# One reciprocal root per up-projection tile on VectorE's side, and TensorE transposes for the second pieces of the latent heads

## The chip, the core and the metric

One core of a Trainium2 chip runs the whole kernel: TensorE (PE; its weight loads are listed as PEld), VectorE (DVE), ScalarE (ACT), GpSimd (POOL) and the SyncE queue (SP), which here issues every transfer. Each engine takes its instructions in the order in which the built program has them. The metric is the time of one execution in device microseconds (us); lower is better. L with a number is a line of the kernel before.

## The reference

One encoder layer over 1024 positions of width 1024. The part that matters is the latent attention (eight heads, keys and queries of 96 values, of which the last 32 are rotated by position):

```
q = jnp.dot(rmsnorm(q_lat, g_q_latent[l]), w_q_up[l]).reshape(B, S, MLA_HEADS, MLA_QK)
kv = jnp.dot(rmsnorm(kv_lat, g_kv_latent[l]), w_kv_up[l]).reshape(B, S, MLA_HEADS, MLA_NOPE + MLA_V)
k_nope, v = kv[..., :MLA_NOPE], kv[..., MLA_NOPE:]
k = jnp.concatenate(
    [k_nope, jnp.broadcast_to(k_rope[:, :, None, :], (B, S, MLA_HEADS, MLA_ROPE))], axis=-1)
q = rmsnorm(q, g_mla_q[l])
k = rmsnorm(k, g_mla_k[l])
q = jnp.concatenate([q[..., :MLA_NOPE], rope(q[..., MLA_NOPE:], positions)], axis=-1)
...
o_mla = mla_attention(q, k, v)
```

`mla_attention` is a causal softmax by chunks of 64 positions: block i of 128 queries sees the keys of blocks 0 to i. A second attention (eight heads, a band of nine chunks, called the chunk heads here) runs beside it; both outputs meet in the output projection, and a gated MLP with a convolution follows.

## The kernel before

The layer runs in stages: input projections and modulation, the chunk heads, the latent heads, output projection, MLP. Positions are cut in eight tiles of 128 (t or i = 0 to 7).

*Precision.* A float32 factor is split in a high and a low part and multiplied in three passes (`gemm3`). Probabilities are split in two f16 parts, each multiplied with the values.

*Up projections* (`f_up`, L519 on). For each of two groups of four heads (gr = 0, 1) and each t: matmuls `qu` into PSUM, copied to SBUF (`uqr`, L553), squared (`usq`, L555), summed by DVE per head (`uss`, L558), and `rsqrt_mean` (L113 to L116) makes the reciprocal root of the mean on POOL in two steps: scale and add (L115), power of -0.5 (L116). DVE multiplies (`qn`, L561) and `rope_apply` rotates the last 32 values in four POOL steps (L467 to L470), with `uqr` for the products. Then matmuls `ku`, and the same for the key: copy `kraw` (L569), the value's two f16 parts (L571, L572), square (L574), sum (`kss`, L577), the rotary part's own sum added by POOL (L578), a second `rsqrt_mean`, DVE for the first 64 values (L581) and POOL for the rotary 32 (L582). `uqr` and `kraw` come from the tag "R", a ring of four buffers.

*Heads* (`Unit`, `mla_unit`). A head has two units, g = 0 for tiles 0 to 3 and g = 1 for tiles 4 to 7. `prep` makes the unit's query and key pages: `qk_page` (L615 on) transposes four blocks on PE into the PSUM tag "T", which has one buffer (TB = 1), and ACT and DVE write the high and low parts. `scores(i)` computes scores into the PSUM tag "S" (two buffers, L658), DVE masks 64x64 of them (L676) and takes the row minimum (L677; signs are turned), ACT takes the exponential (`Pm`, L683) with its sum, DVE the reciprocal (L685, L686). For n keys, `pieces` is one piece up to 640 and two above (0 to 512, 512 to n): tiles 5, 6 and 7 have second pieces of 256, 384 and 512 columns. Each piece goes the same way: POOL scales it to f16 (`hlm`, L71), DVE makes the low part (L703), and a DMA transpose on SP (L705) turns both into `PTm`. The tags "HL" and "PT" have three buffers each. `values(i)` (L716) multiplies all blocks of `PTm` with the values into one PSUM bank per unit; after four tiles ACT and DVE write the unit's output (L723, L724), which goes to memory.

*What sets the order.* The program is emitted in a loop over tiles: `scores` of tile n, then `values` of tile n - 3 (DEPTH = 3), with steps of other work (`fillers`) taken between by `pace`. The fillers are, in order, the projections of the chunk heads, the latent projections, `f_up(0)`, `f_up(1)` and `f_oca`, which projects the chunk heads' output in sixteen tiles (`oc`; loads `cl` and `wor`). A unit of group 0 with g = 1 and all of group 1 need `f_up(1)` done. A scheduler then reorders what is emitted on each engine by dependencies and priorities (`high_priority`). The buffers of a tag go round in the order in which the program asks for them, whatever the scheduler does. The chunk heads' values take the tag "v16", six buffers, which nothing uses once those heads are done. The tiles `P` wider than 640 come from the tag "pg", six buffers, which also hold the latent pages `latT`.

Of the kernel before, what the change touches and what calls it, by code (L numbers as in the profile page):

```python
# [62 lines left out]
def layer_kernel(ctx, tc, I, out):  # L63
# [49 lines left out]
    def rsqrt_mean(r, ss, n, cols=None):  # L113
        sc = ss if cols is None else ss[:, cols]
        pool.tensor_scalar(sc, sc, 1.0 / n, EPS, op0=MUL, op1=ADD)  # L115
        pool.tensor_tensor(r, ss, nhalf[:].to_broadcast(list(r.shape)), op=ALU.pow)  # L116
# [17 lines left out]
    def rtile(name, shape=(P, 512), dt=F32):  # L134
        return apg.tile(list(shape), dt, name=name, tag="R", bufs=4)
# [322 lines left out]

    latT = {}

    def rope_apply(o, x, tab, t, nh, tmp):

        a = tmp[:, 0:nh * 32].rearrange("p (a b) -> p a b", a=nh)
        b = tmp[:, nh * 32:2 * nh * 32].rearrange("p (a b) -> p a b", a=nh)
        ct = tab[:, t:t + 1, 0:32].to_broadcast([P, nh, 32])
        sn = tab[:, t:t + 1, 32:64].to_broadcast([P, nh, 32])
        pool.tensor_tensor(a, x, ct, op=MUL)  # L467
        pool.tensor_tensor(b, x, sn, op=MUL)
        pool.tensor_tensor(o[:, :, 0:16], a[:, :, 0:16], b[:, :, 16:32], op=SUB)
        pool.tensor_tensor(o[:, :, 16:32], a[:, :, 16:32], b[:, :, 0:16], op=ADD)  # L470

    def f_m():
        w = load_w("wm_", I["w_m"], NM)
# [43 lines left out]
    def f_up(gr):  # L517
        if gr == 0:
            right.__exit__(None, None, None)  # L519
            for i in "4v3":  # L520
                G["cm" + i] = tc.tile_pool(name="gp" + i, bufs=1, side="right", reuse_waits="tile")
                G[i] = G["cm" + i].__enter__()
        wq = []
        for k in range(2):
            raw = qtile(f"wqr{gr}_{k}")
            sp.dma_start(raw[:, :384], I["w_qu"][gr][:, k, :])
            w = g4([P, 2, 512], F32R, f"wq{gr}_{k}")
            hi_of("a", w[:, 0, :384], raw[:, :384])
# [12 lines left out]
        lo_of("p", wk[:, 1], raw[:], wk[:, 0])  # L541
        for t in range(NT):
            h, j = divmod(t, 4)
            sl = slice(j * P, (j + 1) * P)
            if t % 2 == 0:
                mq[gr, t // 2] = g3([P, 2, 4, QK], F32, f"qn{gr}_{t}")
                mk[gr, t // 2] = g3([P, 2, 4, QK], F32, f"kn{gr}_{t}")
                mv[gr, t // 2] = G["v"].tile([P, 2, 4, 2, 64], F16, name=f"vt{gr}_{t}", tag="Gv", bufs=8)
            pt = ps.tile([P, 512], F32, name=f"qu{gr}_{t}", tag="mm", bufs=2)
            yield from gemm3_f(pt[:, :384], [(latT[k, h][:, 0, sl], latT[k, h][:, 1, sl], wq[k][:, 0, :384], wq[k][:, 1, :384])  # L550
                                for k in range(2)])
            raw = rtile(f"uqr{gr}_{t}")
            act.activation(raw[:, :384], pt[:, :384], AF.Copy)  # L553
            sq = qtile(f"usq{gr}_{t}")
            act.activation(sq[:, :384], raw[:, :384], AF.Square)  # L555
            ss = cst.tile([P, 4], F32, name=f"uss{gr}_{t}", tag="ss", bufs=4)
            r = cst.tile([P, 4], F32, name=f"ur{gr}_{t}", tag="rr", bufs=4)
# [15 lines left out]
            s3 = raw[:, 256:512].rearrange("p (a b) -> p a b", a=4)  # L573
            act.activation(s3, r3, AF.Square)  # L574
            ss = cst.tile([P, 4], F32, name=f"kss{gr}_{t}", tag="ss", bufs=4)
            r = cst.tile([P, 4], F32, name=f"kr{gr}_{t}", tag="rr", bufs=4)
            dve.tensor_reduce(ss[:], s3, axis=AX.X, op=ADD)  # L577
            pool.tensor_tensor(ss[:], ss[:], ssr[:, t:t + 1].to_broadcast([P, 4]), op=ADD)  # L578
            rsqrt_mean(r[:], ss[:], QK)
            k_t = mk[gr, t // 2][:, t % 2]  # L580
            dve.tensor_tensor(k_t[:, :, 0:NOPE], r3, r[:].unsqueeze(2).to_broadcast([P, 4, NOPE]), op=MUL)  # L581
            pool.tensor_tensor(k_t[:, :, NOPE:], kr[:, t:t + 1, :].to_broadcast([P, 4, ROPE]),  # L582
                               r[:].unsqueeze(2).to_broadcast([P, 4, ROPE]), op=MUL)


    def load_wo(k0, n, he, le):
# [41 lines left out]
    class Unit:  # L628
# [7 lines left out]
        def scores(u, i):  # L636
# [47 lines left out]
            with tc.high_priority(offset=OFF_P):  # L684
# [2 lines left out]
                u.pt[i] = []  # L687
                for x, (p0, p1) in enumerate(pieces):
                    w = p1 - p0
                    hl = at.tile([P, 1280], F16, name=f"hl{nm}_{x}", tag="HL", bufs=HL_BUFS)  # L690
                    pp = pr[:, p0:p1]
                    cnt[0] += 1
                    mode = (MODE_C if u.band else MODE_M)[cnt[0] % 4]
# [4 lines left out]
                    else:  # L698
# [2 lines left out]
                        else:  # L701
                            act.activation(hl[:, :w], pp, AF.Copy, scale=ri[:])
                        dve.scalar_tensor_tensor(hl[:, w:2 * w], pp, ri[:], hl[:, :w], op0=MUL, op1=SUB)  # L703
# [448 lines left out]
```

## Time and profile before

| what | value |
|---|---|
| median of 3 runs | 1462.71 us (1461.91 to 1462.82) |
| the profiled execution | 1464.36 us |
| its span, first to last instruction | 1462.2 us |
| mean granted TensorE clock | 0.934 |
| busy in the span | PE 87%, DVE 69%, POOL 56%, ACT 42% |
| first and last copy of an up projection (L553) | 400.9 and 489.5 us |
| first and last score matmul of the latent heads (L658) | 429.9 and 656.9 us |
| DMA transposes of the latent heads (L705) | 88, median 3.3 us from issue to landing |

A row of a group gives line, engine, operation, output and inputs, shapes, count, then busy time, mean of one in ns, and the idle time before it with what ended it. A row of waits gives who waited for whom, the sum in us, how often, and the longest. A row of the timeline gives start and length in us. A busy PE is not a PE at its peak, since matmuls overlap.

### The profile page before, as it was taken

How to read it: one execution, taken by the hardware profiler on the slowest of the kernel's cores; microseconds unless marked ns; L12 is line 12 of the kernel's file. 1: busy time of each engine (PE TensorE's matmuls, PEld its weight loads, DVE VectorE, ACT ScalarE, POOL GpSimd, SP SyncE). 2: the span in 40 equal slices, each digit the busy share in tenths (PEclk: the TensorE clock that was granted, in tenths of full speed). 3: DMA queues.
4: the chain of work that ended last, by engine and by line, in shares of the span. 5: the costliest groups of instructions: out<-in, count | busy, mean ns of one | idle time of the engine just before them, and what ended most of it. 6: DMA issues, size and time to landing. Idle time of an engine off the chain costs nothing.

```text
span 1462.2 us, 20198 instructions
## 1 busy us (share of the span) xinstructions
PE 1278.0 (87%) x6836; PEld 1058.7 (72%) x6836; DVE 1013.6 (69%) x1734; ACT 611.4 (42%) x1190; POOL 823.0 (56%) x845
## 2 busy tenths in 40 slices
PE   3859989998967788885776999999999998999997
PEld 2759878886756666664655878788888887887885
DVE  6874776476667868872476887777777777566653
ACT  4453354243455545543274434344444433332331
POOL 5263554274599954534644555566655555665662
PEclk9979987999787899996887999999999999999998
DMA  7323647455522577879611322322222244446442
GB/s 281 134 71 74 131 114 148 129 119 120 112 52 51 115 163 156 180 142 253 246 72 59 105 110 101 116 87 87 87 87 83 75 140 164 151 144 238 146 142 101
DMA packets 218595, 185.94 MB, mean 127 GB/s; under 512 B 148086, under 2 KB 183034, under 8 KB 217468
## 3 DMA queue, kind: packets, MB, share of 16 engines
q1 hardware_dynamic: 218492, 184.66, 44.5%
q8 instruction: 54, 0.88, 0.3%
q14 instruction: 49, 0.40, 0.1%
HBM read 121.17 MB, written 28.84 MB: 103 GB/s over the span
## 4 chain that ended last, share of the span: by engine, by line
PE 39%; DMA 17%; DVE 15%; POOL 13%; issue 12%; ACT 3%; SPq 1%; DVEq 0%; POOLq 0%; ACTq 0%
POOL wds L82 5%; DMA aw<-w_ada 5%; PE p L924 4%; PE p L926 4%; PE p L925 4%; DMA wu<-w_up 3%; DMA PTm<-hlm 3%; PE sc L658 2%; PE dnp L1067 2%; PE dnp L1069 2%; PE dnp L1068 2%; PE sm L658 2%; DVE adacc L243 2%; DVE aacc L430 1%; DVE u L1002 1%
## 5 line engine op out<-in xcount | busy, mean ns | idle before, releaser
L82 POOL TENSOR_TENSOR wds<-wd,wds 128x512 fp32r<-128x512 f32 x88 | 154.6, 1777 | 99.0 <-ACT wds L75 99.0
L82 POOL TENSOR_TENSOR wc<-ws,wc 128x512 fp32r<-128x512 f32 x22 | 65.4, 2972 | 137.8 <-ACT wc L75 137.8
L1057 DVE TENSOR_TENSOR wd<-wd,gmbc 128x1024 f32<-128x1024 f32 x44 | 67.5, 1533 | 80.4 <-DMA wd<-w_down 80.4
L1069 PE MATMUL dnp<-wds,g 128*128 128x512 f32 x308 | 118.4, 390 | 4.5 <-DVE g L82 4.5
L1067 PE MATMUL dnp<-wds,g 128*128 128x512 f32 x308 | 119.6, 390 | 1.9 <-DVE xo L1075 1.9
L75 ACT ACTIVATE wds<-wd 128x512 fp32r<-128x512 f32 x88 | 54.8, 624 | 157.3 <-PE dnp L1069 152.2
L1068 PE MATMUL dnp<-wds,g 128*128 128x512 f32 x308 | 119.5, 389 | 0.0
L71 POOL TENSOR_SCALAR hlm<-Pm,rim 128x512 f16<-128x512 f32 (+4 forms) x88 | 61.9, 706 | 70.1 <-DMA PTm<-hlm 55.1
L703 DVE SCALAR_TENSOR_TENSOR hlm<-Pm,rim,hlm 128x512 f16<-128x512 f32 (+4 forms) x88 | 68.0, 777 | 30.1 <-POOL hlm L71 29.7
L71 POOL TENSOR_SCALAR hlc<-Pc,ric 128x640 f16<-128x640 f32 (+2 forms) x64 | 45.3, 710 | 76.9 <-DVE ric L686 41.2
L1015 DVE TENSOR_TENSOR ws<-wu,wu 128x512 f32<-128x512 f32 x22 | 30.7, 1396 | 76.2 <-DMA wu<-w_up 76.2
L82 DVE TENSOR_TENSOR g<-gr,g 128x512 fp32r<-128x512 f32 x44 | 71.9, 1635 | 11.5 <-ACT g L75 11.5
L1001 DVE SCALAR_TENSOR_TENSOR u<-c,pk,u 128x1023 f32<-128x1023 f32 x44 | 77.4, 1765 | 2.0 <-ACT u L1000 2.0
L1036 ACT ACTIVATE u<-u 128x1024 f32<-128x1024 f32 x22 | 23.4, 1063 | 132.1 <-DVE u L1002 132.1
L683 ACT ACTIVATE Pc<-sc,mc 128x640 f32<-128x640 f32 (+2 forms) x64 | 42.1, 659 | 82.5 <-DVE mc L673 62.0
L658 PE MATMUL sm<-mk,mq 96*128 96x512 f32 (+3 forms) x288 | 68.9, 372 | 7.9 <-ACT Pm L683 7.3
L1000 ACT ACTIVATE u<-c,pk 128x1024 f32<-128x1024 f32 x44 | 52.3, 1236 | 56.2 <-DVE c L1032 56.2
L716 PE MATMUL pvm<-PTm,vt 128*128 128x128 f16 x576 | 50.5, 242 | 28.8 <-DMA PTm<-hlm 24.3
L658 PE MATMUL sc<-k,q 64*128 64x512 f32 (+3 forms) x288 | 70.3, 372 | 4.9 <-ACT Pc L683 3.0
L430 DVE SCALAR_TENSOR_TENSOR aacc<-aw,cs,aacc 128x256 f32<-128x256 f32 x84 | 44.9, 535 | 40.6 <-DMA aw<-w_ada 40.0
L716 PEld LDWEIGHTS <-vt 128*128 128x128 f16 x576 | 41.1, 109 | 41.7 <-issue 38.3
L1069 PEld LDWEIGHTS dnp<-wds,g 128*128 128x128 f32 x308 | 57.8, 188 | 17.7 <-DVE g L82 5.7
(368 smaller groups left out, 4342.0 us busy)
## 6 DMA issues: line engine op xcount, KB each, us to landing
wu<-w_up SPq DMA_DIRECT2D x44, 512.0 KB, 4.3
wd<-w_down SPq DMA_DIRECT2D x44, 512.0 KB, 4.7
aw<-w_ada SPq DMA_DIRECT2D x96, 128.0 KB, 2.3
g_d<-u SPq DMA_DIRECT2D x22, 512.0 KB, 2.6
gr<-g_d SPq DMA_DIRECT2D x44, 256.0 KB, 3.7
x<-x SPq DMA_DIRECT2D x16, 512.0 KB, 8.3
adaw<-w_ada_a SPq DMA_DIRECT2D x8, 1024.0 KB, 5.5
wq_r<-w_qk SPq DMA_DIRECT2D x32, 128.0 KB, 2.6
```

Source lines behind the costliest of these rows:

```text
L71: pool.tensor_scalar(o, i, s, 1.0, op0=MUL, op1=MUL)
L82: (pool if eng == "p" else dve).tensor_tensor(o, i, f32(hi), op=SUB)
L430: dve.scalar_tensor_tensor(acc[:], w[:], cs[:, k:k + 1], acc[:], op0=MUL, op1=ADD)
L658: last = pe.matmul(s[:, c:c + w], qpg[rs_, a, q], kpgs[kh][rs_, b, ko:ko + w], start=(a == 0 and b == 0), stop=(a == 1))
L703: dve.scalar_tensor_tensor(hl[:, w:2 * w], pp, ri[:], hl[:, :w], op0=MUL, op1=SUB)
L716: last = pe.matmul(u.pv[:, c], u.vst(j), mov, start=(x == 0), stop=(x == len(todo) - 1))
L924: pe.matmul(pt, sh, pg[:, 0], start=(k == 0), stop=False)
L1001: dve.scalar_tensor_tensor(u[:, 1:], c[:, :S - 1], pk[:, cv + 1:cv + 2], u[:, 1:], op0=MUL, op1=ADD)
L1057: dve.tensor_tensor(raw[:], raw[:], gmbc[:], op=MUL)
L1067: pe.matmul(pts[t][n], sh, w[n][:, 0], start=(j == 0), stop=False)
L1068: pe.matmul(pts[t][n], sh, w[n][:, 1], start=False, stop=False)
L1069: pe.matmul(pts[t][n], sl, w[n][:, 0], start=False, stop=(j == NF - 1))
```

## The change

In `f_up` the query's and the key's sums go into one tile of eight columns and take one `rsqrt_mean`, after the key's sum is complete. The query's product and rotation, and the key's two products, follow it. The rotation, the addition of the rotary sum and the key's rotary product move from POOL to DVE. The latent projection's own rotation (`f_m`) stays on POOL.

In `scores`, a second piece is scaled in place by POOL in float32, transposed on PE in blocks of 128 into a tile of the tag "T" (the one of `qk_page`), copied to f16 by ACT and completed by DVE. It has no "HL" buffer and no DMA transpose. The first piece of a tile with two pieces takes its two buffers from the tag "v16". Tiles with one piece are as before.

```diff
-    def rope_apply(o, x, tab, t, nh, tmp):
+    def rope_apply(o, x, tab, t, nh, tmp, eng=pool):
...
-        pool.tensor_tensor(a, x, ct, op=MUL)
-        pool.tensor_tensor(b, x, sn, op=MUL)
-        pool.tensor_tensor(o[:, :, 0:16], a[:, :, 0:16], b[:, :, 16:32], op=SUB)
-        pool.tensor_tensor(o[:, :, 16:32], a[:, :, 16:32], b[:, :, 0:16], op=ADD)
+        eng.tensor_tensor(a, x, ct, op=MUL)
+        eng.tensor_tensor(b, x, sn, op=MUL)
+        eng.tensor_tensor(o[:, :, 0:16], a[:, :, 0:16], b[:, :, 16:32], op=SUB)
+        eng.tensor_tensor(o[:, :, 16:32], a[:, :, 16:32], b[:, :, 0:16], op=ADD)
...
-            dve.tensor_reduce(ss[:], sq[:, :384].rearrange("p (a b) -> p a b", a=4), axis=AX.X, op=ADD)
-            rsqrt_mean(r[:], ss[:], QK)
-            q_t = mq[gr, t // 2][:, t % 2]
-            dve.tensor_tensor(q_t, raw[:, :384].rearrange("p (a b) -> p a b", a=4),
-                              r[:].unsqueeze(2).to_broadcast([P, 4, QK]), op=MUL)
-            rope_apply(q_t[:, :, NOPE:], q_t[:, :, NOPE:], tabq, t, 4, raw[:, 0:256])
+            ss = cst.tile([P, 8], F32, name=f"uss{gr}_{t}", tag="ss", bufs=4)
+            r = cst.tile([P, 8], F32, name=f"ur{gr}_{t}", tag="rr", bufs=4)
+            dve.tensor_reduce(ss[:, 0:4], sq[:, :384].rearrange("p (a b) -> p a b", a=4), axis=AX.X, op=ADD)
...
             act.activation(r3, p4[:, :, 0:NOPE], AF.Copy)
+            s3 = raw[:, 256:512].rearrange("p (a b) -> p a b", a=4)
+            act.activation(s3, r3, AF.Square)
+            dve.tensor_reduce(ss[:, 4:8], s3, axis=AX.X, op=ADD)
+            dve.tensor_tensor(ss[:, 4:8], ss[:, 4:8], ssr[:, t:t + 1].to_broadcast([P, 4]), op=ADD)
+            rsqrt_mean(r[:], ss[:], QK)
...
-            pool.tensor_tensor(ss[:], ss[:], ssr[:, t:t + 1].to_broadcast([P, 4]), op=ADD)
-            rsqrt_mean(r[:], ss[:], QK)
+            q_t = mq[gr, t // 2][:, t % 2]
+            dve.tensor_tensor(q_t, rq[:, :384].rearrange("p (a b) -> p a b", a=4),
+                              r[:, 0:4].unsqueeze(2).to_broadcast([P, 4, QK]), op=MUL)
+            rope_apply(q_t[:, :, NOPE:], q_t[:, :, NOPE:], tabq, t, 4, rq[:, 0:256], dve)
             k_t = mk[gr, t // 2][:, t % 2]
...
-            pool.tensor_tensor(k_t[:, :, NOPE:], kr[:, t:t + 1, :].to_broadcast([P, 4, ROPE]),
-                               r[:].unsqueeze(2).to_broadcast([P, 4, ROPE]), op=MUL)
+            dve.tensor_tensor(k_t[:, :, NOPE:], kr[:, t:t + 1, :].to_broadcast([P, 4, ROPE]),
+                              r[:, 4:8].unsqueeze(2).to_broadcast([P, 4, ROPE]), op=MUL)
...
-                    hl = at.tile([P, 1280], F16, name=f"hl{nm}_{x}", tag="HL", bufs=HL_BUFS)
+                    if x:
+                        tt = at.tile([P, 10, P], F16, name=f"PT{nm}_{x}", tag="PT", bufs=PT_BUFS)
+                        nk = w // P
+                        scale_pool(pr[:, p0:p1], pr[:, p0:p1], ri[:])
+                        tp = ps.tile([P, 512], F32, name=f"tp{nm}", tag="T", bufs=TB)
+                        for j in range(nk):
+                            pe.transpose(tp[:, j * P:(j + 1) * P], pr[:, p0 + j * P:p0 + (j + 1) * P], ident[:])
+                        th = tt[:, :nk, :].rearrange("p a b -> p (a b)")
+                        act.activation(th, tp[:, :w], AF.Copy)
+                        dve.tensor_tensor(tt[:, nk:2 * nk, :].rearrange("p a b -> p (a b)"), tp[:, :w], th, op=SUB)
+                        u.pt[i].append((tt, lo + p0 // P, nk))
+                        continue
+                    if len(pieces) > 1:
+                        hl = apg.tile([P, 1024], F16, name=f"hl{nm}_{x}", tag="v16", bufs=6)
+                    else:
+                        hl = at.tile([P, 1280], F16, name=f"hl{nm}_{x}", tag="HL", bufs=HL_BUFS)
...
-                    tt = at.tile([P, 10, P], F16, name=f"PT{nm}_{x}", tag="PT", bufs=PT_BUFS)
+                    if len(pieces) > 1:
+                        tt = apg.tile([P, 8, P], F16, name=f"PT{nm}_{x}", tag="v16", bufs=6)
+                    else:
+                        tt = at.tile([P, 10, P], F16, name=f"PT{nm}_{x}", tag="PT", bufs=PT_BUFS)
```

More of the change, by code (lines that the diff above doesn't have):

```diff
@@ L551, in f_up @@
                                 for k in range(2)])
-            raw = rtile(f"uqr{gr}_{t}")
-            act.activation(raw[:, :384], pt[:, :384], AF.Copy)
+            rq = rtile(f"uqr{gr}_{t}")
+            act.activation(rq[:, :384], pt[:, :384], AF.Copy)
             sq = qtile(f"usq{gr}_{t}")
-            act.activation(sq[:, :384], raw[:, :384], AF.Square)
-            ss = cst.tile([P, 4], F32, name=f"uss{gr}_{t}", tag="ss", bufs=4)
-            r = cst.tile([P, 4], F32, name=f"ur{gr}_{t}", tag="rr", bufs=4)
-            dve.tensor_reduce(ss[:], sq[:, :384].rearrange("p (a b) -> p a b", a=4), axis=AX.X, op=ADD)
-            rsqrt_mean(r[:], ss[:], QK)
-            q_t = mq[gr, t // 2][:, t % 2]
-            dve.tensor_tensor(q_t, raw[:, :384].rearrange("p (a b) -> p a b", a=4),
-                              r[:].unsqueeze(2).to_broadcast([P, 4, QK]), op=MUL)
-            rope_apply(q_t[:, :, NOPE:], q_t[:, :, NOPE:], tabq, t, 4, raw[:, 0:256])
+            act.activation(sq[:, :384], rq[:, :384], AF.Square)
+            ss = cst.tile([P, 8], F32, name=f"uss{gr}_{t}", tag="ss", bufs=4)
+            r = cst.tile([P, 8], F32, name=f"ur{gr}_{t}", tag="rr", bufs=4)
+            dve.tensor_reduce(ss[:, 0:4], sq[:, :384].rearrange("p (a b) -> p a b", a=4), axis=AX.X, op=ADD)
             pt = ps.tile([P, 512], F32, name=f"ku{gr}_{t}", tag="mm", bufs=2)
@@ L572, in f_up @@
             dve.scalar_tensor_tensor(v_t[:, :, 1, :], p4[:, :, NOPE:], sc, v_t[:, :, 0, :], op0=MUL, op1=SUB)
[L573 to L578, printed above, removed]
[L579 removed]
+            q_t = mq[gr, t // 2][:, t % 2]
+            dve.tensor_tensor(q_t, rq[:, :384].rearrange("p (a b) -> p a b", a=4),
+                              r[:, 0:4].unsqueeze(2).to_broadcast([P, 4, QK]), op=MUL)
+            rope_apply(q_t[:, :, NOPE:], q_t[:, :, NOPE:], tabq, t, 4, rq[:, 0:256], dve)
             k_t = mk[gr, t // 2][:, t % 2]
[L581 to L583 removed]
+            dve.tensor_tensor(k_t[:, :, 0:NOPE], r3, r[:, 4:8].unsqueeze(2).to_broadcast([P, 4, NOPE]), op=MUL)
+            dve.tensor_tensor(k_t[:, :, NOPE:], kr[:, t:t + 1, :].to_broadcast([P, 4, ROPE]),
+                              r[:, 4:8].unsqueeze(2).to_broadcast([P, 4, ROPE]), op=MUL)
     def load_wo(k0, n, he, le):
```

## The prediction, made before the change ran

> **What bounds the kernel now.** I read the page first for where engines are dense, then the stretches of one stage, then the waits, then single heads on the timeline. Beside the tiles' names, the built program's own order on each engine tells where the change acts: before the first up projection (398 us) and after the attention (680 us) the order is the same in both programs but for a few POOL steps beside the output projection, so all of the effect lies between. I cut that stretch where the next head's first score tile reaches DVE. Columns: stretch, length, busy us (instructions) of PE, weight loads, DVE, ACT, POOL, granted TensorE clock, DMA share, GB/s.
>
> ```profile
> 398.00:502.40 104.40, 74.94 (x399) 59.90 (x397) 79.59 (x207) 58.55 (x140) 98.66 (x180) 0.83 0.33 70
> 502.40:532.40 30.00, 26.86 (x161) 21.29 (x162) 22.22 (x51) 14.13 (x30) 20.85 (x26) 0.91 0.69 155
> 532.40:563.60 31.20, 25.57 (x176) 21.03 (x174) 19.84 (x50) 13.97 (x29) 12.57 (x15) 0.93 0.76 145
> 563.60:588.20 24.60, 20.52 (x142) 16.34 (x142) 21.05 (x52) 14.10 (x29) 13.94 (x15) 0.88 0.79 178
> 588.20:613.70 25.50, 21.11 (x154) 16.59 (x153) 19.87 (x54) 14.45 (x31) 13.85 (x17) 1.00 0.80 162
> 613.70:638.60 24.90, 21.65 (x143) 17.26 (x143) 21.09 (x47) 11.86 (x26) 10.38 (x13) 0.93 0.77 161
> 638.60:680.20 41.60, 25.89 (x204) 21.06 (x202) 22.32 (x56) 14.80 (x31) 17.32 (x20) 0.82 0.77 169
> ```
>
> Row 1 is the up stage: sixteen up-projection tiles and the first two of eight heads. POOL is busy 98.66 of 104.4 us, 94.5%, DVE 76%: POOL bounds it. The six rows below are the other six heads. The first two carry four chunk-output tiles each and take 30.0 and 31.2 us; the next three carry about two and take 25.0 us on average. There PE is the densest (20.5 to 21.7), DVE is close behind, POOL has 11 us to spare. The last head has the drain in it.
>
> ```profile
> POOL hlm L71 <- DMA PTm<-hlm: 55.1, 33, 4.3
> ...
> PE mq_ps L618 <- DVE mk L625: 4.4, 3, 3.0
> ```
>
> The first of these (of the latent tiles) is the longest wait, POOL for an HL buffer that a DMA transpose still reads; POOL is not the bound of those heads, so this is mostly slack. The second is the one that matters below: a page transpose waiting until DVE has emptied PSUM's only "T" bank.
>
> How heads follow each other now, on DVE:
>
> ```profile
> 585.56 1.20 DVE L677 TENSOR_REDUCE mm<-sm 128x1 f32<-128x1024 f32 x1
> 586.69 0.73 DVE L703 SCALAR_TENSOR_TENSOR hlm<-Pm,rim,hlm 128x512 f16<-128x512 f32 x1
> 587.35 0.15 DVE L685 RECIPROCAL rim<-rsm 128x1 f32<-128x1 f32 x1
> 587.50 0.11 DVE L676 MEMSET sm<- 64x64 f32 x1
> 587.53 0.67 DVE L625 SCALAR_TENSOR_TENSOR mk<-mk_ps,gk_m,mk 96x512 fp32r<-96x512 f32 x1
> 588.12 0.14 DVE L686 TENSOR_SCALAR rim<-rim 128x1 f32<-128x1 f32 x1
> 588.18 0.28 DVE L677 TENSOR_REDUCE mm<-sm 128x1 f32<-128x128 f32 x1
> ```
>
> The last tile of one head is reduced at 585.56 and the first of the next at 588.18: 2.6 us, because the next head's pages were transposed while the old head was still being scored. So of a head's 24.6 us, 22.0 lie between its first and last reduction.
>
> **The change, part one: the up projections.**
>
> ```profile
> L116 POOL TENSOR_TENSOR ur<-uss,nhalf 128x4 f32<-128x4 f32 x16 | 16.2, 1010 | 0.2
> L116 POOL TENSOR_TENSOR kr<-kss,nhalf 128x4 f32<-128x4 f32 x15 | 15.4, 1030 | 0.5
> L468 POOL TENSOR_TENSOR uqr<-qn,tabq 128x128 f32<-128x128 f32 x15 | 9.0, 601 | 0.0
> L582 POOL TENSOR_TENSOR kn<-kr,kr 128x128 f32<-128x128 f32 x15 | 8.4, 557 | 0.6
> L467 POOL TENSOR_TENSOR uqr<-qn,tabq 128x128 f32<-128x128 f32 x15 | 7.2, 478 | 0.2
> L469 POOL TENSOR_TENSOR qn<-uqr 128x64 f32<-128x64 f32 x15 | 6.3, 421 | 0.3
> L470 POOL TENSOR_TENSOR qn<-uqr 128x64 f32<-128x64 f32 x15 | 6.0, 401 | 0.0
> L71 POOL TENSOR_SCALAR hlm<-Pm,rim 128x512 f16<-128x512 f32 x7 | 5.5, 786 | 0.3
> L578 POOL TENSOR_TENSOR kss<-kss,ssr 128x4 f32<-128x4 f32 x16 | 4.4, 278 | 0.1
> L115 POOL TENSOR_SCALAR uss<-uss 128x4 f32<-128x4 f32 x16 | 3.6, 228 | 1.4
> ```
>
> Leaving out L71, a tile costs POOL 1.01 + 1.03 + 0.60 + 0.56 + 0.48 + 0.42 + 0.40 + 0.28 + 2 x 0.23 = 5.24 us, 83.8 for sixteen. Afterwards POOL keeps one scale and one power over eight columns, and the chunk heads show that very shape:
>
> ```profile
> 311.88 0.44 POOL L115 TENSOR_SCALAR ss<-ss 128x8 f32<-128x8 f32 x1
> 312.39 1.65 POOL L116 TENSOR_TENSOR r<-ss,nhalf 128x8 f32<-128x8 f32 x1
> ```
>
> 2.09 us, 33.4 for sixteen: POOL loses 50 us of 98.7 and stops being the bound. (One power over eight columns costs 1.65 against 2.04 for two over four: the joint call itself saves little; the moved steps save the rest.) DVE takes them: three of 128x128 (two rotation products, the key's rotary part), two of 128x64, one of 128x4. The nearest DVE row is
>
> ```profile
> L295 DVE TENSOR_TENSOR rt<-pf,pk 128x128 f32<-128x128 f32 x1 | 0.3, 292 | 0.1
> ```
>
> so 5 x 0.29 (the 64-wide at most that) + 0.15 = 1.61 us, 25.8 for sixteen. The other end is POOL's own price, 2.74 us or 43.8; I take 25.8, the same engine and width. Nothing hides it if DVE becomes the bound, and it does: in the built program this stretch holds one head's scores, not two, so DVE's work is 79.6 - 20.8 (one head, mean of the five middle rows) + 25.8 = 84.6 us. At POOL's old density (94.5%) this takes 89.5 us, at DVE's old one (76%) 111. The query's normalisation now also waits for the key's matmul, copy, square and sum, and both raw tiles sit in a ring of four, so full density is unlikely; I take 90%, 94 us: the second head starts at 492 (487.5 to 509). Then seven heads are left, where before six were left at 502.4.
>
> **Part two: the transposes.** 24 of 88 pieces (those past column 512 in tiles 5, 6 and 7 of each head) lose the DMA transpose. Each gets a POOL scale in place (the price of the f16 one), two to four PE transposes, an ACT copy and a DVE subtraction (which replaces L703). PE: 72 transposes at 0.15 (below, four in 0.60) are 10.8 us; ACT 24 x 0.59 or less = 14, in an engine busy 14 of 25 us per head, so hidden. First pieces get six buffers of the chunk heads' V memory, free by then; that removes the 55.1 us of POOL waits, worth nothing while POOL has slack. On SP, which issues all transfers in order, 24 transposes fewer stand before the chunk-output loads.
>
> The cost is the order on the "T" bank. Its one buffer goes round in program order, and the second pieces of a head are emitted before the next head's pages. The built order shows it: every next head's query page stands behind the transposes of tile 7, and its key page on PE also behind the values of tile 7, half of which wait for a DMA transpose. Prices:
>
> ```profile
> 548.82 1.41 PE L716 MATMUL pvm<-PTm,vt 128*128 128x128 f16 x22
> 550.06 0.60 PE L618 MATMUL mk_ps<-ident,kn 128*96 128x128 f32 x4
> 550.41 0.83 PE L658 MATMUL sm<-mk,mq 96*128 96x512 f32 x3
> ```
>
> ```profile
> 587.33 1.10 ACT L683 ACTIVATE Pm<-sm,mm 128x1024 f32<-128x1024 f32 x1
> 588.33 0.19 ACT L683 ACTIVATION_READ_ACCUMULATOR Pm<-sm,mm 128x1 f32 x1
> 588.54 0.69 ACT L723 ACTIVATE sbm<-pvm,vabm 64x512 f32<-64x512 f32 x1
> ```
>
> ```profile
> 595.86 0.59 ACT L621 ACTIVATE mq<-mq_ps 96x512 fp32r<-96x512 f32 x1 [0.30 <-PE sm L658]
> ```
>
> ```profile
> PTm<-hlm SPq DMA_TRANSPOSE x88, 3.3
> ```
>
> From the last reduction of a head to the first of the next, now one chain: reduction 1.20, exponential 1.29, two small DVE steps 0.29, two POOL pieces 1.57, four transposes 0.60, copy 0.59, subtraction 0.67; then the query page 0.60 + 0.59 + 0.67, the key page the same, scores at most 0.83, memset 0.11: 10.9 us. The other end: from POOL's last piece the key page waits for DVE 0.73, landing 3.3 and sixteen value matmuls 1.03 (5.1 in place of the 3.7 above), and on ACT and DVE the head's own output (0.69, about 0.73) stands before its copies: 13.6, before handovers. I take 13.0 in place of 2.6.
>
> The part between first and last reduction can shrink from 22.0, since 52 of 72 value matmuls (3.3 us), two pages (1.2) and six of 24 output matmuls (about 1.7 at 0.28, a third of the 0.83) move into the gap; PE alone would need 20.5 - 6.2 = 14.3. Two score buffers still make each tile wait for the exponential of the tile two before, so I take 18.5. A head is then 31.5 us (25.2 to 35.6).
>
> The Trainium skill (Perfetto Trace Analysis, section Matmuls under Optimizing Tensor Performance) says that independent groups should rotate through PSUM banks, so that emptying one overlaps the next. The wait of mq_ps on DVE above agrees in kind; by that rule seven groups per head on one bank lose their overlap, the loss that this sum prices from rows.
>
> **The sum.** Second head at 492. It carries the four output tiles: 31.5 + 5.6 (30.6 - 25.0) = 37.1. Five heads at 31.5: 157.5. The last to its end: 18.5 + 1.20 + 1.29 + 0.29 + 1.57 + 0.73 + 3.3 + 1.03 + 0.69 + 0.73 = 29.3 at the least, 41.6 as now; I take 33. The attention ends at 719.6 instead of 680.2: +39.4. The profiled execution took 1464.36 us (span 1462.2 and 2.2 around it), 1.65 above the median of the runs, 1462.71: 1503.8 on its own basis, **1502 us** as a median.
>
> **Rivals.**
> *Faster.* One mechanism: PE and not the chain sets the head's period, the fillers close the gap, and POOL's relief is what remains. With the second head at 487.5, heads at 25.0 (30.6 for the first), the last at 29.3: 672.4, -7.8, 1455 us. It decides where the period stays under 24.9 (492 + 5.6 + 33 + 6P = 680.2). For it: PE busy 20.5 to 21.7 of 25 already. Against: the order, in which page transposes can't come sooner. The Trainium skill (VectorE: DVE Perf Modes, section Rules for kernel authors) prefers TensorE to the DMA for 128x128 transposes that may land in PSUM; by that rule alone the change should gain, this 1455. The long DMA wait agrees with it; the shared bank is not in it.
> *Slower, mildly.* The scheduler's fillers hide about half of the gap: period 28, last head 31: 492 + 33.6 + 140 + 31 = 696.6, +16.4, 1479 us. For it: DVE 21 and PE 23 us of work per head would fit in 25.
> *Slower still.* The up stage doesn't shrink (DVE at 76%, 509) and the period is 34, last 38: 756.6, +76, 1539 us. For it: the up chain now goes PE, ACT, DVE, POOL, DVE on both halves.
> *The DMA relief is the effect*: the 55.1 us would have to be on the path; POOL's spare 11 us per head speak against it, and its result is the faster case.
>
> **How the numbers follow.** Forecast 0.58 (own range 1484 to 1522), mild 0.20, faster 0.11, worst 0.11. A measurement tells about 0.2% (3 us) from no change. Faster 0.11, within 0.02 (the low edge of the mild case), slower 0.87. The range leaves out the faster case and half of the worst: 1466 to 1530.
>
> **What would show it.** POOL's rows L467 to L470 and L582 gone to DVE at about 0.29, L116 at 1.65 sixteen times; DVE densest, near 90%, up to about 492; the second head's first reduction there. Then about 13 us, not 2.6, between a head's last reduction and the next's first, mq_ps and mk_ps waiting on DVE and values on DMA in it, PE idle; heads of 31.5. Wrong would be pages ready at once, a period near 25, or DVE steps nearer 0.5 us.

## The result, and the profile after

The changed kernel takes 1517.28 us (median of 4 runs, 1513.75 to 1521.52) where the kernel before, measured beside it, takes 1462.45 (1461.91 to 1462.82): a ratio of 1.0364, 95% interval 1.0343 to 1.0384. The profiled execution is the fastest of the four, 1513.75 us, with a span of 1512.0 (before 1462.2) and a mean granted clock of 0.916 (before 0.934).

The same stretches as in the prediction, in the kernel after, cut again where a head's first score tile is reduced (the columns are the prediction's):

```profile
398.00:485.00 87.00, 61.74 (x331) 48.53 (x330) 79.82 (x256) 50.15 (x118) 48.91 (x53) 0.83 0.28 63
485.00:524.70 39.70, 31.66 (x182) 24.81 (x181) 25.57 (x56) 18.06 (x37) 19.48 (x20) 0.84 0.52 124
524.70:557.90 33.20, 26.56 (x159) 20.76 (x159) 20.12 (x52) 14.02 (x29) 10.13 (x13) 0.81 0.44 94
557.90:593.20 35.30, 27.85 (x159) 22.34 (x159) 20.83 (x51) 16.07 (x33) 15.42 (x17) 0.74 0.53 118
593.20:627.00 33.80, 25.95 (x160) 20.86 (x159) 19.53 (x51) 14.18 (x29) 9.61 (x13) 0.85 0.43 92
627.00:660.90 33.90, 24.81 (x151) 20.21 (x150) 19.23 (x49) 12.94 (x27) 8.38 (x12) 0.76 0.37 77
660.90:697.00 36.10, 27.27 (x159) 21.63 (x159) 19.92 (x49) 14.18 (x29) 9.25 (x13) 0.80 0.40 85
697.00:725.60 28.60, 22.55 (x157) 18.70 (x155) 18.27 (x48) 14.52 (x33) 12.16 (x15) 0.94 0.68 153
```

Row 1: DVE is busy 79.82 of 87 us, 92%, and POOL 48.91, 56%; one head is in it instead of two. In the five middle heads (rows 3 to 7) no engine is dense: PE is busy 25 to 28 us of 33 to 36, DVE 20, POOL 8 to 15, and the DMA share is 0.37 to 0.53 where it was 0.69 to 0.80. Heads take 33 to 36 us. The attention ends at 725.6 instead of 680.2.

The steps that moved, on DVE in 398 to 485 us, and the power that POOL keeps (busy us, mean ns of one, idle before):

```profile
L468 DVE TENSOR_TENSOR uqr<-qn,tabq 128x128 f32<-128x128 f32 x15 | 5.3, 350 | 0.0
L467 DVE TENSOR_TENSOR uqr<-qn,tabq 128x128 f32<-128x128 f32 x15 | 4.9, 324 | 0.0
L579 DVE TENSOR_TENSOR kn<-kr,ur 128x128 f32<-128x128 f32 x15 | 4.2, 282 | 0.0
L469 DVE TENSOR_TENSOR qn<-uqr 128x64 f32<-128x64 f32 x15 | 3.3, 219 | 0.0
L470 DVE TENSOR_TENSOR qn<-uqr 128x64 f32<-128x64 f32 x15 | 3.2, 212 | 0.0
L568 DVE TENSOR_TENSOR uss<-uss,ssr 128x4 f32<-128x4 f32 x16 | 2.4, 152 | 0.1
```

```profile
L116 POOL TENSOR_TENSOR ur<-uss,nhalf 128x8 f32<-128x8 f32 x16 | 26.5, 1654 | 1.1
```

Where a head ends and the next begins, on the timeline (start, length, in brackets the idle time before and its releaser):

```profile
612.10 0.44 PE L694 MATMUL tpm<-ident,Pm 128*128 128x128 f32 x2 [0.81 <-POOL Pm L71]
612.50 1.21 DVE L674 TENSOR_REDUCE mm<-sm 128x1 f32<-128x1024 f32 x1
...
615.70 0.83 PE L732 MATMUL pvm<-PTm,vt 128*128 128x128 f16 x12 [1.07 <-DMA PTm<-hlm]
...
616.35 0.69 POOL L71 TENSOR_SCALAR Pm<-Pm,rim 128x512 f32<-128x512 f32 x1 [0.77 <-DVE rim L683]
616.37 0.50 PE L694 MATMUL tpm<-ident,Pm 128*128 128x128 f32 x3
...
618.13 0.63 PE L694 MATMUL tpm<-ident,Pm 128*128 128x128 f32 x4 [1.27 <-DVE PTm L697]
...
619.43 0.69 DVE L697 TENSOR_TENSOR PTm<-tpm,PTm 128x512 f16<-128x512 f32 x1 [0.78 <-ACT PTm L696]
620.07 1.16 PE L732 MATMUL pvm<-PTm,vt 128*128 128x128 f16 x14 [1.31 <-DMA PTm<-hlm]
621.02 1.06 PE L615 MATMUL mq_ps<-ident,qn 128*96 128x128 f32 x4
...
623.58 0.84 PE L615 MATMUL mk_ps<-ident,kn 128*96 128x128 f32 x4
...
625.33 0.50 PE L655 MATMUL sm<-mk,mq 96*128 96x128 f32 x2 [0.91 <-ACT mk L621]
...
626.97 0.56 DVE L674 TENSOR_REDUCE mm<-sm 128x1 f32<-128x128 f32 x2
```

Tile 7 is reduced at 612.50, the next head's tile 0 at 626.97: 14.5 us instead of 2.6. Between them the second pieces of tiles 6 (616.37) and 7 (618.13), then the next query page (621.02), then its key page (623.58), each after the one before it has left the T bank. Tile 5's piece, too, was transposed only at 612.10. That lateness, and the values (`pvm`) that wait for a DMA transpose in front of a transpose on PE, matter below.

The waits of the whole attention, 398 to 726 us, say the same (who waited for whom, sum, times, longest):

```profile
POOL hlm L71 <- DVE rim L683: 50.4, 17, 12.8
...
PE pvm L732 <- DMA PTm<-hlm: 32.5, 24, 3.4
...
POOL hlm L71 <- DMA PTm<-hlm: 1.1, 1, 1.1
```

POOL's 55.1 us of waiting for DMA are down to 1.1; instead it waits for the next exponential's reciprocal, that is for work.

### The profile page after: what moved, and what is told of

The parts are those of the page before. It is cut to its first block, busy times and chain, and to the rows that moved or that the text cites. A ratio compares the mean times of both kernels' runs of the same rounds, so it can differ in the third digit from the quotient of the medians.

```text
span 1512.0 us, 20231 instructions
## 1 busy us (share of the span) xinstructions
PE 1311.5 (87%) x6908; PEld 1083.6 (72%) x6908; DVE 1026.0 (68%) x1830; ACT 625.1 (41%) x1214; POOL 766.8 (51%) x717
## 4 chain that ended last, share of the span: by engine, by line
PE 24%; POOL 9%; DVE 8%; issue 7%; DMA 6%; ACT 1%; SPq 0%; DVEq 0%; POOLq 0%; ACTq 0%
POOL wds L82 5%; PE p L940 5%; PE p L942 4%; PE p L941 4%; DMA wu<-w_up 2%; PE dnp L1083 2%; PE dnp L1084 2%; PE dnp L1085 2%; DVE u L1018 1%; DMA wd<-w_down 1%; DVE u L1017 1%; POOL wf L82 1%; POOL we L82 1%; DVE ws L1031 1%; DMA PTm<-hlm 1%
## 5 line engine op out<-in xcount | busy, mean ns | idle before, releaser
L71 POOL TENSOR_SCALAR hlm<-Pm,rim 128x128 f16<-128x128 f32 (+3 forms) x64 | 43.9, 686 | 127.9 <-DVE rim L683 50.4
L655 PE MATMUL sm<-mk,mq 96*128 96x512 f32 (+3 forms) x288 | 77.8, 403 | 17.0 <-ACT mk L621 8.8
L732 PE MATMUL pvm<-PTm,vt 128*128 128x128 f16 x576 | 55.6, 255 | 35.9 <-DMA PTm<-hlm 32.5
L732 PEld LDWEIGHTS <-vt 128*128 128x128 f16 x576 | 46.1, 116 | 48.4 <-issue 44.5
L82 DVE TENSOR_TENSOR g<-gr,g 128x512 fp32r<-128x512 f32 x44 | 69.8, 1587 | 11.4 <-ACT g L75 11.4
L655 PEld LDWEIGHTS sm<-mk,mq 96*128 96x128 f32 x288 | 54.2, 219 | 30.8 <-ACT mk L621 12.2
L430 DVE SCALAR_TENSOR_TENSOR aacc<-aw,cs,aacc 128x256 f32<-128x256 f32 x84 | 44.7, 532 | 40.2 <-DMA aw<-w_ada 39.7
```

The lines of the kernel that those rows point to most:

```text
L71: pool.tensor_scalar(o, i, s, 1.0, op0=MUL, op1=MUL)
L82: (pool if eng == "p" else dve).tensor_tensor(o, i, f32(hi), op=SUB)
L655: last = pe.matmul(s[:, c:c + w], qpg[rs_, a, q], kpgs[kh][rs_, b, ko:ko + w], start=(a == 0 and b == 0), stop=(a == 1))
L732: last = pe.matmul(u.pv[:, c], u.vst(j), mov, start=(x == 0), stop=(x == len(todo) - 1))
```

## Experiments

Twelve runs, each against runs of the kernel before on the same chip, whose medians lie between 1464.2 and 1465.7 us there, in a range of some 12 us. The table reads each one's trace at the same points on DVE: when the third head's first tile is reduced (two heads done), the mean period of heads 3 to 7, the mean gap from a head's last reduction to the next head's first over the same five heads, the mean step inside them from tile 3's reduction to tile 4's, and when the last head's output is done.

| kernel | us | ratio to before, 95% | third head | period | gap | tile 3 to 4 | end |
|---|---|---|---|---|---|---|---|
| before | 1462.5 | 1 | 502.4 | 27.3 | 2.7 | 3.0 | 680.2 |
| after | 1517.3 | 1.0364 (1.0343 to 1.0384) | 524.7 | 34.5 | 15.4 | 4.8 | 725.6 |
| up_alone | 1461.4 | 0.9976 (0.9959 to 0.9993) | 503.1 | 26.8 | 3.0 | 2.7 | 679.1 |
| transposes_alone | 1517.7 | 1.0357 (1.0322 to 1.0392) | 531.2 | 33.8 | 16.3 | 4.4 | 731.5 |
| second_bank | 1464.9 | 1.0004 (0.9985 to 1.0022) | 495.5 | 27.7 | 4.4 | 4.2 | 680.9 |
| pages_early | 1485.4 | 1.0140 (1.0108 to 1.0173) | 505.2 | 30.1 | 1.7 | 12.5 | 694.8 |
| both_pages_early | 1490.2 | 1.0156 (1.0120 to 1.0191) | 510.4 | 31.2 | 6.7 | 8.9 | 703.4 |
| last_by_dma | 1503.3 | 1.0270 (1.0233 to 1.0308) | 525.2 | 32.3 | 15.0 | 4.1 | 719.9 |
| last_only | 1507.5 | 1.0305 (1.0275 to 1.0335) | 523.5 | 33.8 | 16.4 | 3.9 | 723.7 |

(The expectations have 15.8 us for the mean gap of the changed kernel, a rougher reading over six boundaries.)

**The two halves.** up_alone has the new `f_up` and the old `scores`, transposes_alone the reverse (edits are shown in short form here and below):

```
 up_alone            f_up: as changed   scores: as before
 transposes_alone    f_up: as before    scores: as changed
```

> The changed up projections with the scores of before: no PE transposes of second pieces, first pieces in their old memory. Theory (one PSUM bank, taken in program order by the second pieces, is what costs): the gap between a head's last and the next head's first reduction goes back to about 3 us and heads to about 25 us (30 with chunk-output tiles). Two heads' scores lie in the up stage again, and with the moved steps DVE has 79.6 + 25.8 = 105 us of work in it: at the 92% seen in the changed kernel it ends near 512 us instead of 502. About 1465 to 1475 us, gap 2 to 4. Rival (the up part carries much of the loss, since its longer chain delays what comes after): over 1490. Second rival (POOL was the bound, its relief is a gain): 1455 or less.

> The changed scores (PE transposes of second pieces, V memory for first pieces) with the up projections of before: rotation on POOL, two powers per tile. Theory (bank order): gaps of 14 to 19 us between heads stay, periods of 33 to 36 us, POOL about 95% busy in the up stage; 1505 to 1525 us, about what both parts together gave. Rival (the two parts share the loss): 1480 to 1495. Second rival (the transfers taken from the DMA queue are a gain once POOL is not also relieved): 1460 or less.

The up projections alone are a little faster than before, 0.9976, and faster than their expectation of 1465 to 1475 us; the transposes alone carry the whole loss, 1.0357 of 1.0364, with the same gaps, as expected. Of up_alone, from the stage's start to the third head, as in the first row of the prediction:

```profile
398.00:503.10 105.10, 75.49 (x416) 60.22 (x416) 95.03 (x302) 61.75 (x145) 61.38 (x60) 0.82 0.36 76
```

POOL has fallen from 98.66 to 61.38 us and the stage ends 0.7 us later: DVE, with 95.03 instead of 79.59, is its bound at 90%. The expectation had 105 us of DVE work and the stage's end at 512. It added the rows of the moved steps to the busy time, but DVE's steps overlap in the trace, so that a row is longer than what it adds:

```profile
410.56 0.28 DVE L467 TENSOR_TENSOR uqr<-qn,tabq 128x128 f32<-128x128 f32 x1
410.76 0.28 DVE L468 TENSOR_TENSOR uqr<-qn,tabq 128x128 f32<-128x128 f32 x1
```

The second of these starts 0.20 us after the first, which is listed with 0.28. All DVE rows of the stage sum to 91.4 us before and to 115.1 us in up_alone, 23.7 more, while the busy time grows by 15.4.

**The bank.** second_bank takes the transposes' PSUM tile from the two buffers of the projections; pages_early changes only where the next head's first pages are emitted, and both_pages_early moves the second pages too:

```
-  tp = ps.tile([P, 512], F32, name=f"tp{nm}", tag="T", bufs=TB)
+  tp = ps.tile([P, 512], F32, name=f"tp{nm}", tag="mm", bufs=2)      # second_bank
```

```
+  if i == 5 and not u.band: prep() of the next head's unit g = 0, ahead of scores(5)      # pages_early
+  if i == 7 and not u.band: prep() of its unit g = 1, ahead of tile 7's pieces            # both_pages_early
```

> The changed kernel with the second pieces' transposes put into the two PSUM buffers that the projections use, instead of the T bank; their number and cost are the same. Theory (order of the bank): next head's pages are free again, gap about 3 us, periods 25 to 28 us; in the built order 19 reductions instead of 10 stand ahead of the last up tile, so the up stage ends later, near 512 us. Total 1455 to 1475 us. Rival (transposes and copies as such): periods over 31 us, total over 1495 us. Second rival (the projections' buffers only move the wait): gaps near 3 but an up stage and chunk-output heads that are longer by the 12 us that a gap had; total about 1485 us.

> The changed kernel with one thing moved: the next head's first query and key pages are emitted ahead of tile 5 of a head's second half, before the second pieces of tiles 5, 6 and 7 take the T bank. Nothing is added or left out. Theory (order of the bank): the mean gap falls from 15.8 to 3 to 6 us, periods to 25 to 28 us, total 1455 to 1475 us. Rival (the work itself, PE transposes with their copies and subtractions, or the slower clock, makes a head long): gaps shrink but periods stay over 31 us, total over 1495 us.

> As the run with early first pages, and the next head's second query and key pages now come ahead of tile 7's second piece. Nothing is added or left out. In the run with early first pages the wait between heads (1.6 to 1.8 us) had come back inside the head, 9 to 14 us between the reductions of tiles 3 and 4. Theory (whatever stands behind the second pieces on the T bank waits for them): that inner gap falls to 3 to 6 us, heads to 23 to 26 us, total 1455 to 1470 us. Rival (the head is then held by something else, for example values that wait for a transpose, or PE itself): heads stay at 27 to 31 us, total 1475 to 1488 us.

second_bank settles the main question. The same 72 transposes with the same copies and subtractions, in another place, cost little: 1.0004 instead of 1.0364, gaps of 4.4 us, as expected (only the up stage did not get longer: the third head starts at 495.5, not near 512). They are not free. Against up_alone, which has none of them and ran on the same chip, second_bank is 3.5 us slower in the median; the means of ten runs each differ by 3.8 us, with a 95% interval of 1.5 to 6.2. bank_four and up_four (below), the same pair with one buffer more in the output projection, differ by 4.3 in the mean (1.2 to 7.3). The two of a pair also differ in the buffers of the first pieces, so the 0.3% is not the transposes' alone for certain. And second_bank gives the transposes two buffers as well as other company; which of the two counts was not separated. Its heads 5 and 6 take 22.0 and 22.3 us, under the 24.5 and 25.5 of before (head 6 also has fewer output matmuls, 10 instead of 29), but heads 3 and 4, with 36 and 42 output matmuls that use the same two buffers, take 34.6 and 32.2.

pages_early brings the gap to 1.7 us, under that of before, and yet only some 60% of the loss back: its expectation was too hopeful. Its timeline in the next head shows where the wait went:

```profile
544.02 0.61 PE L694 MATMUL tpm<-ident,Pm 128*128 128x128 f32 x4
...
544.80 0.69 DVE L674 TENSOR_REDUCE mm<-sm 128x1 f32<-128x512 f32 x1
...
547.06 0.60 PE L615 MATMUL mq_ps<-ident,qn 128*96 128x128 f32 x4
...
551.63 0.40 PE L152 MATMUL oc<-wo,cl 128*128 128x512 f32 x1
551.87 0.60 PE L615 MATMUL mk_ps<-ident,kn 128*96 128x128 f32 x4
...
554.35 0.61 PE L732 MATMUL pvm<-PTm,vt 128*128 128x128 f16 x8 [1.88 <-DMA PTm<-hlm]
...
556.62 0.82 DVE L674 TENSOR_REDUCE mm<-sm 128x1 f32<-128x640 f32 x1
```

The old head's tile 7 is transposed at 544.02, when tile 3 of the new head is about to be reduced (544.80); the new head's second pages follow at 547.06 and 551.87, and tile 4 at 556.62. What stands behind the pieces waits for them, now inside the head (12.5 us instead of 3.0). But only 3.0 us lie between the old tile's transposes and the new query page. Most of the rest lies between the two pages and behind them: ahead of the key page PE has scores, values and six output matmuls, of which the last is shown, and ahead of tile 4's scores values that wait 1.88 us for DMA. With both pairs of pages moved the step from tile 3 to 4 shrinks to 8.9, but the gap is 6.7 again and the time no better: this expectation missed, and what else holds those heads at 31 us I did not find. The order on one bank can be shifted, but no order tried is free.

**One piece of the three.** last_by_dma gives tile 7's second piece back to DMA, last_only gives back tiles 5 and 6:

```
-  if x:
+  if x and i < 7:       # last_by_dma
+  if x and i == 7:      # last_only
```

> The changed kernel, but tile 7's second piece goes by DMA as before; tiles 5 and 6 keep their PE transposes, so two thirds of these pieces and 40 of the 72 transposes stay. Theory (the loss is what stands last ahead of the next head's pages on the T bank): the next head's pages now wait for tile 6 alone, which is done about when tile 7 is reduced; the mean gap falls from 15.8 to 4 to 8 us, heads to 26 to 29 us, total 1465 to 1485 us. Rival (each PE transpose costs its share, in work or in hold-ups): two thirds of the loss stay, 1495 to 1502 us, gaps over 10.

> The mirror of it: only tile 7's second piece is transposed by PE, tiles 5 and 6 go by DMA as before; 32 of the 72 transposes stay. Theory (tile 7 stands last ahead of the next head's pages): the gaps stay at 12 to 16 us and most of the loss with them, total 1495 to 1515 us. Rival (each transpose costs its share): 45% of the loss, about 1487 us, with gaps of 7 to 9.

The second came out as expected; the first did not. Without tile 7 the gap is still 15.0 us and three quarters of the loss remain, near the rival's two thirds; but that rival gives last_only 45%, and 84% remain there. In last_by_dma, around tile 7's reduction at 608.96, what leads to tile 6's transposes:

```profile
608.55 0.44 PE L694 MATMUL tpm<-ident,Pm 128*128 128x128 f32 x2 [0.91 <-POOL Pm L71]
608.96 1.21 DVE L674 TENSOR_REDUCE mm<-sm 128x1 f32<-128x1024 f32 x1
...
610.94 0.72 PE L732 MATMUL pvm<-PTm,vt 128*128 128x128 f16 x10 [1.95 <-DVE om L740]
...
611.47 0.71 PE L150 MATMUL oc<-wo,ch 128*128 128x512 f32 x1
...
612.11 0.59 POOL L71 TENSOR_SCALAR Pm<-Pm,rim 128x384 f32<-128x384 f32 x1
...
613.69 0.63 PE L152 MATMUL oc<-wo,cl 128*128 128x512 f32 x1
...
614.12 1.25 PE L732 MATMUL pvm<-PTm,vt 128*128 128x128 f16 x12
...
615.20 0.50 PE L694 MATMUL tpm<-ident,Pm 128*128 128x128 f32 x3
...
616.87 0.64 PE L615 MATMUL mq_ps<-ident,qn 128*96 128x128 f32 x4 [1.17 <-DVE PTm L697]
```

Tile 6 holds the pages as long: its piece comes at 615.20, 6.2 us after tile 7's reduction. For the first 3.7 us it is not ready: POOL has scaled it by 612.70, after a reciprocal that stood behind tile 7's reduction on DVE. For the other 2.5 us PE is not free: the piece stands behind the values of tiles 4 and 5 (10 and 12 matmuls), the first of which wait 1.95 us until DVE has emptied the values' own PSUM bank, and behind six output matmuls between them (611.47 to 614.12), which are fillers. In the changed kernel above, the values ahead wait for DMA (1.07 at 615.70). The pages inherit all this through the T bank. So the loss is neither a share per transpose (40 of 72 cost 2.7%, 32 of 72 cost 3.05%, all 3.6%) nor tile 7's: one piece ahead of the pages is nearly enough. That the values and output matmuls ahead add to tile 6's lateness is read from this timeline; no run took them away.

**Smaller terms.** up_balanced is up_alone with three of the moved steps left on POOL; up_vmem is up_alone with first pieces in the V memory; up_vmem_pace6 adds a faster pace of fillers; up_four is up_alone, and bank_four second_bank, with a fourth buffer in the output projection:

```
+  pool.tensor_tensor(o[:, :, 0:16], ...), (o[:, :, 16:32], ...), (k_t[:, :, NOPE:], ...)   # up_balanced
-  if x:  ... PE transposes ...                                              # up_vmem: by DMA, from "HL"
-  R_CA, R_MLA = 1.9, 0.5
+  R_CA, R_MLA = 1.9, 0.6                                                    # up_vmem_pace6
-  lo, hi = gb.tile(..., tag="ol", bufs=3), gb.tile(..., tag="oh", bufs=3)
+  lo, hi = gb.tile(..., tag="ol", bufs=4), gb.tile(..., tag="oh", bufs=4)   # up_four, bank_four
```

> The changed up projections with the scores of before, but three of the six moved steps a tile stay on POOL: the rotation's subtraction and sum and the key's rotary product. In the run of the up projections alone DVE was busy 65.2 of 74.2 and 29.8 of 31.0 us (95.0 to 503.1) and POOL 61.4, before it was POOL 98.7 and DVE 79.6 to 502.4. Theory (the stage goes by the denser of the two, the work was only moved from one to the other): DVE gives back 16 x 1.0 = 16 us at the most and POOL takes 16 x 1.4 = 22, so both stand near 80 to 85 us, the stage ends near 490 to 495 us and the total is 1449 to 1456 us. Rival (the stage goes by the chain from matmul to normalised key, or by PE): it ends at 500 to 505 us whatever the split, total 1459 to 1465 us.

> The changed up projections, all pieces transposed by DMA as before, but first pieces in the six buffers of the V memory: the changed kernel without its PE transposes. Theory (buffers alone are worth nothing, POOL has slack there): POOL's wait for DMA before its pieces falls from 42.8 us to under 20, and the time is that of the up projections alone within 3 us, 1458 to 1464 us. Rival (that wait was on the path): heads of 22 to 23 us and 1452 us or less.

> As the run with the V memory and without PE transposes, with the pace of fillers in the latent heads at 0.6 instead of 0.5, so that the last chunk-output tile is issued some 270 PE instructions ahead of the attention's end instead of behind it. In that run the attention ended at 658.5 us, 20 us earlier than with the up projections alone, but the last chunk-output tiles ran at 663 and the last output weights arrived at 686, as in the kernel before. Theory (six more buffers for first pieces do shorten heads, and the output weights, which wait for the chunk output's weights to be done with, hide it): attention ends at 660 to 668 us, output weights are in by then, total 1446 to 1454 us. Rival (the earlier end was only work pushed behind it): attention ends at 675 to 680 us, total 1458 to 1464 us.

> The changed up projections with the scores of before, and in the output projection four buffers instead of three for the attention output and its high half, so that the fourth tile's copy no longer stands behind the squares of the first tiles on ACT. Theory (the 6.5 us of PE's wait there before, 10.8 us in the changed kernel, are that copy): PE's wait goes under 2 us and the time falls by 4 to 8 us against the up projections alone, 1453 to 1457 us. Rival (PE waits for PSUM to be emptied by DVE anyway, three output banks): no more than 2 us less, 1459 to 1462 us.

> The changed kernel with its transposes in the projections' two PSUM buffers, and the same four buffers in the output projection. Theory (the 4.4 us that the changed kernel lost after the attention are the fourth tile's copy): the output matmuls take 55 to 58 us from first to last instead of 63.9, total 1455 to 1460 us. Rival (PSUM of the output projection sets it): 62 to 64 us and 1463 to 1466 us in all.

| kernel | us | ratio to before, 95% |
|---|---|---|
| up_balanced | 1464.0 | 0.9991 (0.9975 to 1.0008) |
| up_vmem | 1463.7 | 0.9983 (0.9961 to 1.0005) |
| up_vmem_pace6 | 1463.4 | 0.9998 (0.9982 to 1.0014) |
| up_four | 1461.2 | 0.9981 (0.9963 to 0.9999) |
| bank_four | 1466.7 | 1.0011 (0.9991 to 1.0031) |

up_balanced: the third head starts at 499.0 us instead of 503.1, not at 490 to 495, and the time is that of before; the expectation missed. Up to that start POOL is busy 78.43 us, near the 80 to 85 foreseen, but DVE 90.84 instead of 95.03: it gave back 4.2 us, not up to 16. The three rows that left it sum to 11.7 us in up_alone, of which a part overlapped, and one step that it kept became longer. First up_alone, then up_balanced, 398 to 503 us (shortest, median and longest in ns):

```profile
L578 DVE TENSOR_TENSOR kn<-kraw,ur x15: 396/415/829, 410.0 to 494.8; 128x256 f32<-128x256 f32 x15
```

```profile
L578 DVE TENSOR_TENSOR kn<-kraw,ur x16: 410/540/831, 406.6 to 501.4; 128x256 f32<-128x256 f32 x16
```

up_vmem: POOL's wait for DMA falls from 42.8 to 21.0 us, not quite under the 20 expected (6.6 in up_vmem_pace6), and the time is up_alone's within the spread, as expected of buffers that relieve an engine with slack. Its profiled execution, the fastest of its ten (1456.1 us), even ends the attention at 659.3 us, 20 earlier, but with the last chunk-output tiles behind it, and PE then waits 9.63 us for output weights:

```profile
673.50 1.65 PE L150 MATMUL op<-wo,oh 128*128 128x512 f32 x3 [9.63 <-ACT wo L75]
```

up_vmem_pace6 has those tiles inside the attention; it then ends at 675.3, and the time does not move: that end was work pushed behind it, the rival of that run. up_four and bank_four: the output matmuls shrink in the profile from 61.4 to 56.2 us and from 63.9 to 58.8, and the medians move by less than 2 us. PE's wait there for the fourth tile's copy falls to 4.1 and 2.7 us from 8.6 (up_alone) and 8.8 (second_bank), not under 2. Both expectations missed; up_four ends that stage 6.7 us earlier than up_alone (737.0 instead of 743.7), of which 3.6 are left when the down projection begins (1199.8 instead of 1203.4), and with runs that spread over 12 us the rest can't be told.

No version beats the kernel before by more than 0.24% (up_alone), which is near the edge of what a run can tell.

## Why the prediction was right, point by point

*POOL stops being the bound, DVE becomes it: right.* The power of eight columns took 1.654 us (1.65 foreseen), the six moved steps 1.54 us a tile by their rows (0.350, 0.324, 0.282, 0.219, 0.212, 0.152; 1.61 foreseen), DVE's density was 92% (90% taken). The second head began at 485.0 instead of 492, with 79.8 us of DVE work ahead of it, not 84.6. A wrong step in that sum is known: it added the moved steps' row times to busy time, and row times count the overlap of DVE's steps twice (see up_alone, where 25.8 us were added and the busy time grew by 15.4). How much of the difference this makes here was not split. The prediction treated this as a gain of time; up_alone shows that it is hardly one. With two heads in the stage, as before, the third starts at 503.1 instead of 502.4. The earlier stage end of the changed kernel is one head less in it: after one head before stands at 471.2, and the changed kernel at 485.0.

*The next head's pages wait on the T bank: right, and shown by second_bank.* The gap was mis-sized: 13.0 was taken with 13.6 at the top, the five gaps have a mean of 15.4. The chain was counted from tile 7's reduction, with each engine free when its turn comes but for the values and the head's output. In the trace tiles 5 and 6 are late too (612.10, 616.37 against a reduction at 612.50), and last_by_dma shows that tile 7 could be left out of the chain with hardly a change. And PE's prices were those of an undisturbed clock. Two of the five gaps, those with the highest and the lowest granted clock:

```profile
612.50:626.97 14.47, 9.63 (x83) 8.17 (x83) 7.00 (x17) 5.76 (x10) 4.25 (x5) 0.88 0.53 108
...
643.75:660.93 17.18, 10.10 (x75) 8.87 (x74) 8.07 (x16) 4.87 (x9) 3.02 (x4) 0.62 0.32 62
```

The five gaps have 0.70, 0.68, 0.88, 0.62 and 0.77, the scores of the same heads 0.79 to 0.90; whole heads (3 to 7) had 0.88 to 1.00 before and 0.74 to 0.85 here. PE was foreseen idle in the gap; it is busy for 9.1 to 11.2 us of each.

*The score part of 18.5 us: nearly right*, a mean of 19.1. So a head is 34.5 us where 31.5 was forecast, inside the range given for it (25.2 to 35.6). The first head with four output tiles took 39.7 (37.1), the last 28.6 (33; the tail of 29.3 was nearly the truth). By terms: -7.0 for the stage, +2.6, 5 x 2.96 = +14.8, -4.4, together +6.0 on an attention end of 719.6: 725.6 as measured. That the end came so near is in part luck: the heads were too short by 17.4 us in all, the stage and the last head too long by 11.4.

*Nothing changes behind the attention: wrong.* The span grew by 49.8 us, the attention's end by 45.4. The order on the engines in the output projection differed more than by a few POOL steps: ahead of the first `x`, DVE has three sums and two products of `pa` before, and three of each after. The fourth tile's copy stands on ACT behind squares that wait for POOL and DVE, and PE waits for it, first before, then after:

```profile
708.96 0.80 PE L150 MATMUL op<-wo,oh 128*128 128x512 f32 x1 [6.53 <-ACT oh L75]
```

```profile
760.87 0.80 PE L150 MATMUL op<-wo,oh 128*128 128x512 f32 x1 [10.83 <-ACT oh L75]
```

That is 4.3 of the 4.4 us in the profile; bank_four removes most of the wait, and its time shows no gain, so what the 4.4 us are worth in a median stays open.

*The relief of POOL's waits for DMA is worth nothing: right* (up_vmem, up_vmem_pace6). *The rivals*: mild (1479) would have needed fillers in the gap; the five gaps hold 7, 4, 6, 1 and 2 output matmuls, of 19 to 25 a head, and most of what PE does there belongs to the chain. Faster (1455) needed pages that come in time. second_bank nearly gives that (gaps of 4.4 us), and its 1464.9 is no gain: beyond the bank the transposes bring nothing. By the Trainium skill (VectorE: DVE Perf Modes, Rules for kernel authors) a 128x128 transpose belongs on TensorE where PSUM can take it; the runs add that it gains nothing here even so. Its other rule (Perfetto Trace Analysis, Optimizing Tensor Performance, Matmuls), to rotate independent groups through PSUM banks, comes near to second_bank, which takes one group of users off the shared buffer: 1517.3 us on the T bank, 1464.9 on others. That one the runs bear out.

## What to carry to other kernels

Before a transpose or a matmul is given a PSUM tag that others use, list who comes behind it in program order and what the newcomer waits for: all of them inherit its waits, and one newcomer a head cost nearly as much as three (3.05% and 3.6%). If the profile shows no engine dense at a boundary and the gap as a chain across PE, ACT and DVE, try the same work in another bank before its order or its amount. Work moved off the bounding engine gains only if the receiver has room for it: here POOL's 37 us went and DVE's 15 us came, for the same stage. And what a moved step adds is read from busy time, not from the sum of its rows.

## What was not expected of the hardware

The granted clock was lower with the long gaps: 0.62 to 0.88 in them and 0.79 to 0.90 in the scores between, where whole heads before had 0.88 to 1.00. Score matmuls took a mean of 401 ns against 367 (heads 5 to 7, all shapes together). Yet PE is busy for 59 to 74% of a gap, and its longest wait in the five is 2.7 us. The Trainium skill (TensorE: Matmul & The Clock Gate, HAM oscillation) tells of a clock throttled again when PE idles for more than about 3.4 us; no wait of that length stands in these gaps, so that rule alone does not account for them, and what lowers the clock stays open.

DVE's 128x256 product took a median of 540 ns instead of 415 with three steps a tile back on POOL. A busy POOL alone is not the reason, since before, with POOL busy for 94.5% of the stage, the median was 417. The means of two other steps rose as well, DVE's 128x4 sum from 152 to 259 ns and POOL's power from 1656 to 1897, but by two and three long ones among sixteen: their medians are 148 and 161, 1642 and 1646. What the engines share there was not tried.
